# A two-way gated delta-rule scan on one core: queries, keys and state scaled ahead of the products, and sums left to PSUM

## The chip, the core and the metric

The kernel runs on one core of a Trainium2 chip. The core has a matrix engine (PE) that writes to PSUM, a vector engine (DVE), an activation engine (ACT), a third elementwise engine (POOL, which here works on SBUF tiles only) and a queue that issues transfers (SP). Each engine takes its instructions in the order in which they were written out when the program was built, and they meet at semaphores. The metric is the device time of one execution in microseconds.

## The reference

One layer of a hybrid backbone over 256 context and 1024 latent tokens of width 1024. A shared projection feeds two groups: a gated delta rule with four heads of 128, run forwards and backwards, and a neighbourhood attention with eight heads of 64. Both go through one output projection, and a gated feed-forward block follows. The change touches the recurrence of the delta rule:

```python
    def step(S, xs):
        q_i, k_i, u_i, w_i, qk_i, gam_i = xs
        v_new = u_i - jnp.einsum("bhck,bhkv->bhcv", w_i, S)
        o_i = (jnp.einsum("bhck,bhkv->bhcv", q_i * jnp.exp(gam_i)[..., None], S)
               + jnp.einsum("bhcm,bhmv->bhcv", qk_i, v_new))
        g_last = gam_i[..., -1:]
        k_dec = k_i * jnp.exp(g_last - gam_i)[..., None]
        S = S * jnp.exp(g_last)[..., None] + jnp.einsum("bhck,bhcv->bhkv", k_dec, v_new)
        return S, o_i
```

`u` is the inverse of a triangular matrix times the values, `w` the same inverse times the decayed keys. The state `S` is 128x128 for each head and direction.

## The kernel before

Tokens are cut into ten chunks of 128 (the first two are context). The forward scan takes them in order, the backward scan as 1, 0, 9, 8, ... 2; a step i of the program is one chunk of each direction, so there are ten steps with twenty chunk scans. What depends on no state was made earlier and lies in memory: `y_d` (the triangular inverse), `at_d` (decayed query-key products), keys in both layouts (`kT_d`, `k_d`), queries (`qT_d`) and values (`v_d`). `load` (L267) fetches six tiles of 256 KB for a latent chunk, for both directions at the start of the step before.

`scan` (L1181) is a generator. In each chunk it computes K S (`kT` and `s`), subtracts the values after scaling by `EG` (L1193, one DVE instruction per head), multiplies by the inverse (`vn` and `y`), scales the result twice: on ACT to `vk` for the state (L1214, one per head), and on DVE to `vn` for the output (L1216). The output is a sum of queries times state, scaled by `EG` and written out per head (L1207 on ACT when the latent chunk is met first, L1204 on DVE when it is met the second time), and of `at` times `vn` (L1223). The new state is the old one times `ET` plus `kt` times `vk` (L1233, one per head). A chunk that both directions have passed is normalised, gated and split into two parts by `finish` (L1242). Each direction's context chunks give no output, its last chunk no state.

A product of two 128x128 tiles of f32 goes to PE as two passes, so four heads show as eight instructions in the trace. PSUM holds two accumulators of 128x512 for the scan (tag `ps`) and two larger ones for the attention (tag `sc`).

Beside the scan runs the neighbourhood attention (`attention`, L287): 32 blocks of two heads, here called pairs. Of a pair, PE makes the scores (`kh`, `kl` with `qs`), DVE adds the bias and takes the maximum (L338), ACT the exponential (L341), DVE normalises (L343), PE transposes (the ten products of `bt` with `cst`), ACT copies to `pt` (L351), PE multiplies by the values (`vc`, `vw`), and ACT and DVE split the result (L363, L364). POOL clears the context columns of a bias tile `bt` (L304), and SP loads the rest (L305). A bias tile can be cleared only when its former transposes are done.

The order of the two is written out by hand. The main loop (L1303 on) asks the two scans in turn for a piece; after each piece `beside(PACE)` adds 0.72 to a count, and for each full unit of it the attention goes on by one of its yields (two per pair, 67 in all). The list so made is then put in order for each engine by a scheduler that works with modelled times. In the last step, the remaining attention and the first products of the output projection (`two_blocks`, the tiles `ew`) are written out.

## Time and profile before

| | us |
|---|---|
| median of three runs | 1526.46 |
| lowest and highest | 1523.25, 1526.57 |
| span of the profiled execution (its first to last instruction) | 1527.5 |
| PE, DVE, ACT, POOL busy in that span | 1462.8, 1013.5, 707.1, 184.1 |
| the stage in which the scan runs | 558 to 800 |

The profile shows one execution; its page gives no time for it beside the span, which is 1.0 us above the median of the runs. Matmuls and transposes are called from two helper lines (L99, L103), so the names of tiles tell them apart: `ps` are the scan's, `sc` the attention's. [...] The chain of waits follows the work that ended last back through whatever released it. A releaser named in a row is the one that came last by the profile.

### The profile page before, as it was taken

How to read it: one execution, taken by the hardware profiler on the slowest of the kernel's cores; microseconds unless marked ns; L12 is line 12 of the kernel's file. 1: busy time of each engine (PE TensorE's matmuls, PEld its weight loads, DVE VectorE, ACT ScalarE, POOL GpSimd, SP SyncE). 2: the span in 40 equal slices, each digit the busy share in tenths (PEclk: the TensorE clock that was granted, in tenths of full speed). 3: DMA queues.
4: the chain of work that ended last, by engine and by line, in shares of the span. 5: the costliest groups of instructions: out<-in, count | busy, mean ns of one | idle time of the engine just before them, and what ended most of it. 6: DMA issues, size and time to landing. Idle time of an engine off the chain costs nothing.

```text
span 1527.5 us, 23479 instructions
## 1 busy us (share of the span) xinstructions
PE 1462.8 (96%) x8365; PEld 1209.5 (79%) x8365; DVE 1013.5 (66%) x1908; ACT 707.1 (46%) x1379; POOL 184.1 (12%) x251
## 2 busy tenths in 40 slices
PE   6999998899999989999899999999999999999998
PEld 3789787678877778887787888788888888888887
DVE  4886579455687427679976488766565656599652
ACT  5443461574366536666643284333333334354441
POOL 0153500243134300000100000000000000000000
PEclk9999999999999999999999999999999999999999
DMA  9377133565477789998529404433333335798742
GB/s 368 110 235 231 58 86 122 184 179 179 131 216 252 222 266 277 279 273 247 170 65 317 166 35 163 134 104 103 104 104 103 104 104 166 252 367 288 235 152 83
DMA packets 209829, 276.28 MB, mean 181 GB/s; under 512 B 15968, under 2 KB 116912, under 8 KB 208688
## 3 DMA queue, kind: packets, MB, share of 16 engines
q1 hardware_dynamic: 208992, 274.41, 56.0%
q8 instruction: 66, 1.08, 0.3%
q14 instruction: 51, 0.42, 0.1%
q10 hardware_dynamic: 720, 0.37, 0.1%
HBM read 209.93 MB, written 68.98 MB: 183 GB/s over the span
## 4 chain that ended last, share of the span: by engine, by line
PE 65%; DVE 8%; DMA 6%; ACT 5%; issue 2%; SPq 1%; POOL 0%; POOLq 0%; ACTq 0%; DVEq 0%
PE ps L99 44%; PE blk L99 10%; PE sc L99 4%; PE pr L99 3%; DMA nv_d<-zt 2%; PE sc L103 2%; PE m L99 1%; DMA wraw<-w_nqk 1%; DMA wad<-wa 1%; ACT bt L341 1%; DVE bt L338 1%; DVE ulo L1418 1%; ACT pt L351 1%; DVE x L1587 1%; SPq L1065 0%
## 5 line engine op out<-in xcount | busy, mean ns | idle before, releaser
L99 PE MATMUL ps<-hT,uhi 128*128 128x512 f32 x496 | 146.8, 390 | 1.5 <-DVE e L1708 1.4
L99 PE MATMUL ps<-lT,uhi 128*128 128x512 f32 x496 | 146.4, 389 | 0.0
L99 PE MATMUL ps<-hT,ulo 128*128 128x512 f32 x496 | 146.2, 389 | 0.0
L99 PE MATMUL blk<-hh,whi 128*128 128x512 f32 (+1 forms) x456 | 139.1, 397 | 2.0 <-ACT hh L720 1.3
L99 PE MATMUL blk<-hh,wlo 128*128 128x512 f32 (+1 forms) x456 | 130.1, 378 | 0.0
L99 PE MATMUL blk<-hl,whi 128*128 128x512 f32 (+1 forms) x456 | 129.3, 377 | 0.0
L99 PE MATMUL ps<-hB,uhi 128*128 128x512 f32 x436 | 129.1, 390 | 0.0
L99 PE MATMUL ps<-lB,uhi 128*128 128x512 f32 x436 | 128.8, 389 | 0.0
L99 PE MATMUL ps<-hB,ulo 128*128 128x512 f32 x436 | 128.7, 389 | 0.0
L1417 ACT CAST uhi<-wq 128x512 fp32r<-128x512 f32 x101 | 60.3, 621 | 132.8 <-PE ps L99 67.7
L1417 ACT CAST uhi<-ws 128x512 fp32r<-128x512 f32 x91 | 54.7, 622 | 144.8 <-PE ps L99 77.5
L1418 DVE TENSOR_TENSOR ulo<-wq,uhi 128x512 fp32r<-128x512 f32 x101 | 67.2, 687 | 65.4 <-ACT uhi L1417 38.5
L99 PEld LDWEIGHTS ps<-hT,uhi 128*128 128x128 f32 x496 | 93.0, 188 | 21.3 <-ACT uhi L1417 1.8
L99 PEld LDWEIGHTS ps<-lT,uhi 128*128 128x128 f32 x496 | 93.0, 188 | 19.7 <-DVE lT L1571 0.5
L99 PEld LDWEIGHTS ps<-hT,ulo 128*128 128x128 f32 x496 | 93.1, 188 | 19.4
L99 PEld LDWEIGHTS ps<-hB,uhi 128*128 128x128 f32 x436 | 81.9, 188 | 17.4 <-issue 0.5
L99 PEld LDWEIGHTS ps<-lB,uhi 128*128 128x128 f32 x436 | 81.8, 188 | 17.3 <-DVE lB L1571 0.4
L99 PEld LDWEIGHTS ps<-hB,ulo 128*128 128x128 f32 x436 | 81.9, 188 | 17.0
L99 PEld LDWEIGHTS blk<-hh,wlo 128*128 128x128 f32 x456 | 80.9, 191 | 17.9 <-issue 2.5
L99 PEld LDWEIGHTS blk<-hl,whi 128*128 128x128 f32 x456 | 81.0, 190 | 15.4
L99 PEld LDWEIGHTS blk<-hh,whi 128*128 128x128 f32 x456 | 77.7, 193 | 19.4 <-ACT hh L720 3.1
L338 DVE CUSTOM_DVE_ANT_0 bt<-sc,bt 128x640 f32<-128x640 f32 x64 | 52.5, 822 | 50.3 <-issue 38.7
(337 smaller groups left out, 3073.0 us busy)
## 6 DMA issues: line engine op xcount, KB each, us to landing
wq<-w_fo SPq DMA_DIRECT2D x99, 256.0 KB
wq<-w_gu SPq DMA_DIRECT2D x88, 256.0 KB
wad<-wa SPq DMA_DIRECT2D x64, 256.0 KB
bt<-rpb SPq DMA_DIRECT2D x64, 192.0 KB
t_d<-g SPq DMA_DIRECT2D x22, 512.0 KB
fr<-t_d SPq DMA_DIRECT2D x44, 256.0 KB
f_d<-g SPq DMA_DIRECT2D x33, 256.0 KB
fr<-f_d SPq DMA_DIRECT2D x33, 256.0 KB
```

The costliest lines, as they stand in the source:

```text
L99: i = nc.tensor.matmul(*args, **kw)
L103: i = nc.tensor.transpose(*args, **kw)
L338: dve.tensor_tensor_reduce(bt, sc[:, u * 640:u * 640 + 640], bt, 1.0, -3.0e38, OP.add, OP.max, m[:, 0:1])
L341: act.activation(bt, bt, AF.Exp, bias=m[:, 1:2], accum_out=m[:, 2:3])
L351: act.copy(pt, sc[:, u * 640:u * 640 + 640])
L1417: act.copy(hi, self.raw[key])
L1418: dve.tensor_tensor(lo, self.raw[key], hi.bitcast(F32), OP.subtract)
L1587: dve.tensor_tensor(B[at][:, k], B[x][:, k], B.get(y, B["B11"])[:, k], OP.subtract)
```

## The change

The recurrence is written in another way. `w`, the inverse times the decayed keys, is made as a tile of its own one step ahead (`before`): POOL scales the keys by `EG` to `ke`, PE multiplies `ke` with `y`, ACT copies the result with its sign turned to `w`. In the scan, `y` times `v` and `w` times `s` then add up in one accumulator `z`, and one DVE instruction scales it by `B` for all four heads to `vn`, which serves both the output and the state. POOL also scales the keys by `KD` (in place), the queries by a row of decays `er` (which SP loads broadcast over partitions and ACT exponentiates) and the state by `ET` to `sd`. Queries times state and `at` times `vn` add up in one accumulator. The tables `KN` and `KB`, the loads of `kT` and the tile `vk` go. The state tile of a direction is one buffer that is written over.

The forward scan's pieces are written out before the backward scan's, `before` for the next step beside them, and `finish` as a third party; each piece says by its yield how much it counts, and PACE is 1.25. Values and `at` of the next step are fetched between the two scans. Buffers: `kt`, `y`, `qT` four, `er` two, `at` three.

```diff
-PACE = 0.72
+PACE = 1.25
...
+        kt, y = (own.tile([128, 4, 128], F32, name=n, tag=f"{n}{d}") if own else
+                 scan_in.tile([128, 4, 128], F32, name=n, tag=n, bufs=4) for n in ("kt", "y"))
+        sp.dma_start(fl(kt), k_d[c * 128:(c + 1) * 128])
+        sp.dma_start(y, y_d[d, c])
+        qT = er = None
+        if c >= 2:
+            qT, er = (scan_in.tile([128, 4, 128], F32, name=n, tag=n, bufs=2 if n == "er" else 4)
+                      for n in ("qT", "er"))
+            u = (d * NCH + c) * 4
+            sp.dma_start(fl(er), g_d[u:u + 4].rearrange("h t -> (h t)").partition_broadcast(128))
+            sp.dma_start(qT, qT_d[:, :, (c - 2) * 128:(c - 1) * 128])
+        ready[d, c] = kt, qT, er, y
+
+    def load_values(d, c, own=None):
...
-                KN, KB = (fw.tile([128, 2, NCH, 4], F32, name=n, tag=n, bufs=1) for n in ("KN", "KB"))
-                dve.tensor_tensor(KN, KD, NB, OP.mult)
-                dve.tensor_tensor(KB, KD, B, OP.mult)
...
+        def before(d, c):
+
+            kt, qT, er, y = ready[d, c]
+            carried = c != ORDER[d][0]
+            if carried:
+                ke = work("ke", 1)
+                pool.tensor_tensor(ke, kt, spread(EG, d, c), OP.mult)
+            if c >= 2:
+                act.activation(er, er, AF.Exp)
+                pool.tensor_tensor(qT, qT, er, OP.mult)
+            yield 0.0
+            if carried:
                 p = bank()
                 for h in range(4):
-                    pe.matmul(p[:, hs[h]], kT[:, h], s[:, h], start=True, stop=True)
+                    pe.matmul(p[:, hs[h]], ke[:, h], y[:, h], start=True, stop=True)
+                made[d, c] = w = work("w")
+                act.activation(fl(w), p, AF.Copy, scale=-1.0)
+            if c != last[d]:
+                pool.tensor_tensor(kt, kt, spread(KD, d, c), OP.mult)
+            yield 0.5
+
+        def scan(d, c):
+            kt, qT, er, y = ready.pop((d, c))
+            v, at = values_of.pop((d, c))
+            lat, s = c >= 2, S[d]
+            vn = work("vn")
+            z = bank()
+            for h in range(4):
+                pe.matmul(z[:, hs[h]], y[:, h], v[:, h], start=h == 0, stop=s is None, skip_group_check=True)
+            if s is not None:
+                w = made.pop((d, c))
+                if c != last[d]:
+                    sd = work("sd", 1)
+                    pool.tensor_tensor(sd, s, spread(ET, d, c), OP.mult)
                 for h in range(4):
...
+                    pe.matmul(z[:, hs[h]], w[:, h], s[:, h], start=False, stop=True, skip_group_check=True)
+            dve.tensor_tensor(vn, z.rearrange("p (h i) -> p h i", h=4), spread(B, d, c), OP.mult)
             if lat:
                 p = bank()
                 for h in range(4):
-                    pe.matmul(p[:, hs[h]], at[:, h], vn[:, h], start=True, stop=True)
-                dve.tensor_tensor(o, p.rearrange("p (h i) -> p h i", h=4), o, OP.add)
+                    pe.matmul(p[:, hs[h]], qT[:, h], s[:, h], start=h == 0, stop=False, skip_group_check=True)
+            yield 1.0
+            if lat:
+                for h in range(4):
+                    pe.matmul(p[:, hs[h]], at[:, h], vn[:, h], start=False, stop=True, skip_group_check=True)
+                o = oacc[:, c - 2]
+                if c in seen:
+                    dve.tensor_tensor(fl(o), p, fl(o), OP.add)
+                else:
+                    act.copy(fl(o), p)
             if c != last[d]:
                 p = bank()
                 for h in range(4):
-                    pe.matmul(p[:, hs[h]], kt[:, h], vk[:, h], start=True, stop=True)
...
+                    pe.matmul(p[:, hs[h]], kt[:, h], vn[:, h], start=True, stop=True)
+                if s is None:
+                    S[d] = s = work("s%d" % d, 1)
+                    act.copy(fl(s), p)
+                else:
+                    dve.tensor_tensor(fl(s), p, fl(sd), OP.add)
...
+            def both():
+                yield from scan(0, ORDER[0][i])
+                if i + 1 < NCH:
+                    for d in range(2):
+                        load_values(d, ORDER[d][i + 1])
+                yield from scan(1, ORDER[1][i])
+
+            main = both()
+            live = [main]
+            if i + 1 < NCH:
+                live.append(chain(*(before(d, ORDER[d][i + 1]) for d in range(2))))
+            while live or ending:
+                live += ending
+                ending.clear()
                 nxt = []
...
+                for g in live:
+                    n = next(g, None)
+                    if n is not None:
                         nxt.append(g)
...
+                        beside(PACE * n)
```

How the instructions move is shown at three places. On DVE in an early step, before (`vn` and `s` are the scan's, `mx`, `bt` and `na` the attention's):

```order
L1233 SCALAR_TENSOR_TENSOR s_6148<-s_5854,ET,ps 128x128
L342 RECIPROCAL mx<-mx 128x1
L340 TENSOR_SCALAR mx<-mx 128x1
L1233 SCALAR_TENSOR_TENSOR s_6148<-s_5854,ET,ps 128x128
L343 TENSOR_SCALAR bt<-bt,mx 128x640
L1233 SCALAR_TENSOR_TENSOR s_6148<-s_5854,ET,ps 128x128
L342 RECIPROCAL mx<-mx 128x1
L1233 SCALAR_TENSOR_TENSOR s_6148<-s_5854,ET,ps 128x128
L343 TENSOR_SCALAR bt<-bt,mx 128x640
L364 TENSOR_TENSOR na_4919<-sc,na_4919 128x8x16
L1193 SCALAR_TENSOR_TENSOR vn<-ps,EG,v 128x128 x4
```

and of the change (L349 to L354 are the softmax's lines there):

```order
L354 TENSOR_SCALAR bt<-bt,mx 128x640
L1232 TENSOR_TENSOR vn<-ps,B 128x512
L353 RECIPROCAL mx<-mx 128x1
L354 TENSOR_SCALAR bt<-bt,mx 128x640
L375 TENSOR_TENSOR na_4911<-sc,na_4911 128x8x16
L1254 TENSOR_TENSOR s_4986<-ps,sd 128x512
L349 ISA bt,mx<-sc,bt 128x640
```

Where four pieces of the state stood between the pieces of a softmax, one instruction for four heads stands now.

On PE in an early step of the change, from the products that make `w` to the first product that reads `vn`; rows of the attention's scores and value products are left out:

```order
L100 MATMUL ps<-y,ke 128x128
L104 MATMUL sc<-cst,bt 128x128 x5
L100 MATMUL ps<-y,ke 128x128
...
L100 MATMUL ps<-y,ke 128x128 x2
...
L100 MATMUL ps<-v,y 128x128 x4
L100 MATMUL ps<-s_5070,w 128x128 x4
L100 MATMUL ps<-s_5070,qT 128x128 x4
L104 MATMUL sc<-cst,bt 128x128 x5
...
L100 MATMUL ps<-vn,at 128x128
```

The product `ke` times `y` belongs to the next step; the three products after it stand together, and transposes of the attention lie between the last of them and the products that read `vn`.

On POOL, in the same stretch of the change, where before a row of 54 clears of `bt` stood alone (`L304 MEMSET bt 128x256 x54`):

```order
L1229 TENSOR_TENSOR sd<-s_5070,ET 128x512
L315 MEMSET bt 128x256
L1202 TENSOR_TENSOR ke<-kt,EG 128x512
L1214 TENSOR_TENSOR kt<-kt,KD 128x512
L1205 TENSOR_TENSOR qT<-qT,er 128x512
L315 MEMSET bt 128x256 x2
L1205 TENSOR_TENSOR qT<-qT,er 128x512
L1229 TENSOR_TENSOR sd<-s_4986,ET 128x512
```

Clears of bias tiles, which wait for the attention's transposes, now stand between the scan's scalings.

103 lines of the change are left out of this document (31 added, 72 removed).

## The prediction

> **What bounds the kernel now.** I read first the busy time by stage (columns: stretch, its length, then busy us and instructions of PE, weight loads, DVE, ACT and POOL, granted clock, DMA share, GB/s). All edits lie in the stage from 558 to 800 us, where the recurrence of the scans ("scan" below) runs beside 32 pairs of attention blocks. Behind it PE is busy 99%.
>
> ```profile
> 558.00:800.00 242.00, 224.77 (x2039) 191.66 (x2038) 191.56 (x687) 151.44 (x412) 21.98 (x62) 1.00 0.78 222
> 830.00:1527.00 697.00, 692.09 (x3060) 571.31 (x3058) 451.04 (x712) 275.53 (x470) 0.00 (x0) 1.00 0.46 156
> ```
>
> PE looks 93% full here, which would leave 17 us. The groups of the stage and pieces of the chain of waits (start, us, what) say otherwise:
>
> ```profile
> L99 PE MATMUL ps<-vn,y 128*128 128x128 f32 x144 | 21.3, 283 | 0.8 <-DVE vn L1216 0.5 <-ACT oacc L1207 0.3
> 754.75 1.79 PE ps L99 x16
> 758.25 0.55 PE sc L103 x5
> 668.57 1.79 PE sc L99 x26
> 787.30 7.85 PE sc L99 x34
> ```
>
> A scan product is recorded with 283 ns, yet sixteen pass in 1.79 us, 0.112 each: the rest is pipeline. By this pace the stage needs, of PE: 688 scan products x 0.112 = 77; a pair takes ten transposes (2 x 0.55), twenty value and six score products (1.79) and four more score products (about 0.5), 3.4 us, x 32 = 109; 48 products of the output projection x 0.231 = 11; 32 transposes x 0.11 = 4. That is 201 us: PE waits 41 of 242, not 17. DVE is at 79%, the next fullest.
>
> Where the waits lie, the steps of the scan show (step 2 to step 8, one row each, same columns), and the chain inside one early and one late step:
>
> ```profile
> 594.00:617.40 23.40, 22.38 (x200) 18.98 (x200) 16.16 (x54) 14.21 (x40) 1.76 (x6) 1.00 1.07 300
> 617.40:640.30 22.90, 22.33 (x200) 18.90 (x200) 16.32 (x54) 14.01 (x40) 2.05 (x7) 1.00 0.95 267
> 640.30:665.00 24.70, 24.15 (x216) 20.82 (x216) 17.30 (x56) 15.26 (x43) 1.97 (x7) 1.00 0.90 263
> 665.00:688.20 23.20, 21.54 (x201) 18.74 (x202) 18.40 (x62) 12.10 (x29) 1.94 (x6) 1.00 1.08 284
> 688.20:721.10 32.90, 29.44 (x288) 25.24 (x287) 30.51 (x117) 22.05 (x61) 3.11 (x10) 1.00 0.85 246
> 721.10:754.70 33.60, 30.22 (x291) 25.44 (x290) 30.49 (x118) 22.69 (x62) 3.70 (x11) 1.00 0.66 193
> 754.70:785.00 30.30, 27.61 (x266) 23.36 (x266) 27.87 (x108) 18.94 (x51) 3.85 (x8) 1.00 0.32 92
> ```
>
> ```profile
> by line: PE ps L99 38.4%; PE sc L99 24.2%; ACT oacc L1207 10.0%; ACT bt L341 8.5%; PE sc L103 8.4%; ACT pt L351 5.6%; ACT vk L1214 3.7%; issue 3.6%
> 632.33 1.10 PE ps L99 x8
> ...
> 633.72 0.62 ACT oacc L1207 x2
> ...
> 636.25 0.81 ACT bt L341 x2
> ...
> 638.16 0.82 ACT bt L341 x2
> ...
> 639.24 1.04 ACT oacc L1207 x4
> ...
> 640.32 0.38 PE ps L99
> by line: PE ps L99 25.5%; PE sc L99 24.3%; PE sc L103 16.5%; DVE bt L338 5.7%; ACT pt L351 5.6%; issue 3.3%; ACT vk L1214 3.1%; PE ps L103 3.0%; DVE bt L343 2.7%; DVE oacc L1204 2.3%; ACT bt L341 1.6%; DVE s L1233 1.5%; POOL bt L304 1.0%; D
> ```
>
> The first "by line" row is 617.4 to 640.4, the second 729.4 to 763. Early, 71% of a step (16.3 of 23 us) is PE; from 633.4 on, PE waits for ACT, which carries eight `oacc` and eight `vk` evictions, one per head, among the exponentials. Late, 69% (23.3 of 33.6) is PE and DVE is busy 91%. So neither engine is full for long; the waits come where a scan eviction in pieces and the attention's softmax share a queue.
>
> **The change part by part.** The groups that fall and those by which the new ones are priced:
>
> ```profile
> L1193 DVE SCALAR_TENSOR_TENSOR vn<-ps,EG,v 128x128 f32<-128x128 f32 x72 | 21.5, 341 | 1.2 <-PE ps L99 1.1
> L1233 DVE SCALAR_TENSOR_TENSOR s<-s,ET,ps 128x128 f32<-128x128 f32 x64 | 19.0, 342 | 3.8 <-PE ps L99 3.7
> L1204 DVE SCALAR_TENSOR_TENSOR oacc<-ps,EG,oacc 128x128 f32<-128x128 f32 x32 | 9.8, 341 | 0.0
> L1223 DVE TENSOR_TENSOR oacc<-ps,oacc 128x512 f32<-128x512 f32 x16 | 11.0, 687 | 5.9 <-PE ps L99 5.9
> L1216 DVE TENSOR_TENSOR vn<-ps,NB 128x512 f32<-128x512 f32 x16 | 10.9, 684 | 1.0 <-ACT vk L1214 0.8
> 691.58 1.12 DVE L1233 SCALAR_TENSOR_TENSOR s<-s,ET,ps 128x128 f32<-128x128 f32 x4 [0.17 <-PE ps L99]
> L1214 ACT ACTIVATE vk<-ps,KN 128x128 f32<-128x128 f32 x64 | 19.4, 373 | 3.1 <-PE ps L99 3.1
> L1207 ACT ACTIVATE oacc<-ps,EG 128x128 f32<-128x128 f32 x32 | 9.8, 392 | 2.5 <-PE ps L99 2.5
> L1263 ACT CAST gah<-z 128x512 fp32r<-128x512 f32 x8 | 4.9, 613 | 7.4 <-DVE z L1262 7.3
> L1288 POOL TENSOR_TENSOR ew<-ew 128x512 fp32r<-128x512 f32 x2 | 2.6, 1282 | 3.3 <-ACT ew L1287 3.3
> L304 POOL MEMSET bt<- 128x256 f32 x60 | 19.4, 324 | 212.9 <-PE sc L103 139.1 <-PE sc L99 22.1 <-DMA qs<-nq_d 6.7
> SPq L305 <- PE sc L103: 26.7, 30, 2.8
> ```
>
> DVE: 168 pieces go, four in 1.12 us, so 47 us, and 32 whole tiles, 22; there come 20 `vn`, 16 state updates and 8 output sums, 44 x 0.69 = 30. DVE falls by 39 us, from 79% to 63% of the stage.
>
> ACT: 104 pieces, about 31 us, go; 18 `w`, 16 exponentials of `er`, 8 output and 2 state copies come, 44 x 0.61 (a 128x512 cast) = 27. The exponentials are off the path, a step ahead. Only the pieces' dispatch and their place among the softmax change.
>
> PE: the 72 products of keys and state give way to 72 of `w` and state; 72 products `ke` x `y`, two passes each, are new: 144 x 0.112 = 16.1 us, on the engine that carries most of the chain. This is the price.
>
> POOL: 18 `ke`, 18 `kt`, 16 `qT` and 16 `sd` tiles, 68 x 1.28 = 87 us, beside 19 us of clearing bias tiles: 44% of the stage, and all one step ahead except `sd`. Inside a step `sd` has as cover the products and eviction of `vn` of its own chunk (16 products, 1.8 us, and 0.69), and a step is 22 us while a chunk's own recurrence (`w` products 0.9, `vn` 0.7, `kt` products 0.9, state 0.7) is about 3.5. If POOL were late by more than that cover, the state update would wait, and behind it on DVE the next softmax.
>
> DMA: 20 loads of `kT` go, 16 of `er` come, 256 KB each: 1 MB less of 54 MB (222 GB/s x 242 us), four SP issues fewer. Costed at nothing: SP's longest wait in the scan (the last row: total, times, longest) is for a bias buffer that PE still reads, not for an issue; four buffers for `kt`, `y`, `qT` cover the earlier start.
>
> PACE: attention advances per `beside` unit. Before, an early step makes 8 x 0.72 = 5.76 calls and a late one 14 x 0.72 = 10.1; now 5 x 1.25 = 6.25 and 6 x 1.25 = 7.5; two calls are a pair.
>
> The sum, against the profiled 1527.5 us (1.0 above the median of the runs, within their spread), step by step. I assume that half of the chain's waits stay; the bounds are all and none.
> - Steps 3 to 5: PE 16.3 + 16 products x 0.112 = 1.8 + a quarter pair, 0.8 = 18.9; waits 6.7, half is 3.3: 22.2 each, 66.6 for 70.8: -4.2.
> - Steps 6 to 8: PE 23.3 + 1.8 - 1.29 pairs x 3.4 = 20.7; waits 10.3, half 5.2: 25.9 each, 77.7 for 96.8: -19.1.
> - Step 2: 2.6 us of added work against a wait of 6.74 us for a bias load (below): 0.
> - Steps 0 and 1: 1.2 pairs and 32 products more, 7.7; half falls into a wait of 4.91 us that stays (below): +3.9.
> - Step 9: attention has 67 calls; 63.3 were made before it, now 60, so 1.65 pairs more run there, 5.6, and 1 us of their own wait: +6.6.
>
> Together -12.8. The same half taken on the whole stage gives less: 201 + 16.1 + 20.5 = 238 for 242, -4. The steps know where the waits are, the stage counts all of PE's work; I take a value between, nearer the steps: **-10, 1517 us**.
>
> ```profile
> 600.41 6.74 DMA bt<-rpb
> 553.58 4.91 DMA zT_d<-zt
> ```
>
> The recorded PE time alone would give another sum: 17 us idle, 16 filled, so 1 us of gain at most. [...]
>
> **The rivals.**
>
> *The attention keeps its waits, and the new products come on top (slower).* Place: PE's queue, where transposes stand for the softmax on DVE and value products for the copy on ACT. For it: ACT sheds only 4 us, and early steps wait as much with DVE at 71% as late ones at 91%. Against: ACT's own evictions in the early chain go, and the added products lie in those waits. The assumed waits of steps 3 to 8 are 3 x 6.7 + 3 x 10.3 = 51 us; every tenth more that stays costs 5. From -10 the sign turns when more than 0.7 of them stay; at nine tenths it is +10, **1537 us**.
>
> *POOL's queue sets the step.* Its tensor products share something with DVE:
>
> ```profile
> 169.91 1.05 POOL L877 TENSOR_TENSOR rc<-GH,cst 128x512 fp32r<-128x512 f32 x1
> ...
> 173.36 2.22 DVE L899 TENSOR_TENSOR WK<-WK,cst 128x1280 f32<-128x1280 f32 x1
> 174.19 2.29 POOL L877 TENSOR_TENSOR rc<-GL,cst 128x512 fp32r<-128x512 f32 x1
> ```
>
> Alone 1.05, beside a DVE product of two SBUF tiles 2.29. At 2.29, eight per step and six bias clears are 20.3 us, under 22; clears also hold the queue until old transposes are done (139.1 us of waiting in the row of L304). With 0.7 us more per instruction the step is 26: +4 x 6, **1541 us**. Against it: of DVE's scan instructions now all read PSUM, not two SBUF tiles.
>
> [...]
>
> *The early half is DMA's.* The DMA share is 0.90 to 1.08 in steps 2 to 5, with 263 to 300 GB/s. If those cannot shrink, 66.6 becomes 70.8: -6, **1521 us**. Against: one bias load alone stands on the chain.
>
> *It does not do what it says*: scan and attention were independent, attention's chain sets the pace, the added products fill gaps: **1527 us**.
>
> **How the numbers follow.** Forecast 0.58, waits stay 0.15, DMA 0.12, no effect 0.08, POOL 0.07. A measurement of this kernel tells about 0.3% (4.6 us) from no change. Faster: 0.54 of the forecast's, 0.06 of DMA's, 0.01 else, 0.61; same: 0.04, 0.06, 0.06, 0.02, 0.18; slower 0.21. With no waits left in steps 3 to 8 it would be 25 less than with half, which PE's own 217 us forbid before 1503; with nine tenths 1537. The range is 1503 to 1534; the forecast's own 1507 to 1522.
>
> **What would show it.** Right: steps 6 to 8 of 24 to 27 us where 30 to 34 stood; steps 3 to 5 of 21 to 23; DVE near 153 us and PE's need by pace (217 us) at 0.93 of the stage. `ke` and `sd` on POOL near 1.3 us. Wrong: DVE, ACT or PE idle before `ps` with POOL as releaser; early steps of 24 or more with transposes waiting for `bt`; `er` or `at` loads on the chain; or a tail after the last scan product of more than 6 us without PE work.

## The result and the profile after

The changed kernel takes 1544.8 us (median of 4 runs, 1539.78 to 1545.63), the kernel before 1524.86 us (4 runs). The ratio is 1.0127, with a 95% interval of 1.0105 to 1.0149: the change makes the kernel 16 to 23 us **slower**, where 10 us faster was forecast. The profiled execution took 1544.56 us (span 1542.4). That of the kernel before has a span of 1527.5, above all four of its times, so the profiles show about 5 us less of the loss than the medians.

All of what the profiles show lies in the stage of the scans. The busy time by step, from the first whole-tile `vn` eviction of a step (L1232; before, L1216) to that of the next (columns: stretch, its length, then busy us and instructions of PE, weight loads, DVE, ACT and POOL, granted clock, DMA share, GB/s), steps 2 to 9, first the changed kernel:

```profile
592.10:616.30 24.20, 22.54 (x219) 20.28 (x218) 13.55 (x38) 13.59 (x28) 9.47 (x13) 1.00 0.93 269
616.30:645.50 29.20, 26.64 (x240) 23.79 (x239) 16.40 (x46) 15.72 (x32) 14.41 (x19) 0.94 0.86 245
645.50:670.10 24.60, 22.49 (x218) 20.45 (x218) 14.97 (x38) 14.22 (x30) 10.78 (x14) 1.00 0.93 274
670.10:692.50 22.40, 22.36 (x218) 20.45 (x217) 13.49 (x39) 12.00 (x26) 10.38 (x14) 1.00 1.01 264
692.50:726.60 34.10, 28.15 (x266) 24.44 (x266) 27.52 (x85) 20.25 (x53) 11.43 (x16) 1.00 0.64 192
726.60:758.70 32.10, 27.70 (x265) 24.05 (x264) 26.82 (x81) 16.82 (x48) 10.17 (x15) 1.00 0.59 182
758.70:785.20 26.50, 25.57 (x246) 22.44 (x245) 23.35 (x80) 16.96 (x48) 6.61 (x10) 1.00 0.41 123
785.20:814.90 29.70, 28.99 (x221) 24.51 (x220) 18.46 (x64) 12.39 (x37) 0.62 (x2) 1.00 0.15 41
```

The same marks in the kernel before:

```profile
593.40:616.80 23.40, 22.14 (x201) 18.73 (x199) 16.16 (x54) 14.21 (x39) 2.00 (x6) 1.00 1.07 299
616.80:639.70 22.90, 22.38 (x203) 18.95 (x202) 16.32 (x55) 14.01 (x39) 2.00 (x6) 1.00 0.95 271
639.70:659.60 19.90, 19.53 (x169) 16.66 (x170) 14.15 (x47) 11.02 (x31) 1.69 (x5) 1.00 0.90 259
659.60:682.90 23.30, 21.31 (x205) 18.90 (x205) 17.44 (x58) 13.21 (x34) 1.95 (x6) 1.00 1.04 272
682.90:715.80 32.90, 29.44 (x281) 24.66 (x280) 30.34 (x118) 21.65 (x61) 3.11 (x10) 1.00 0.89 255
715.80:749.50 33.70, 30.60 (x294) 25.91 (x292) 30.48 (x118) 22.73 (x62) 3.11 (x10) 1.00 0.73 220
749.50:780.80 31.30, 28.33 (x273) 23.81 (x274) 29.60 (x116) 20.73 (x57) 4.74 (x9) 1.00 0.37 104
780.80:799.80 19.00, 19.00 (x121) 16.23 (x121) 13.26 (x47) 6.90 (x24) 0.00 (x0) 1.00 0.05 15
```

Compare the lengths: steps 3 to 5 grew from 66.1 to 76.2 us, steps 6 to 8 fell only from 97.9 to 92.7, and the last stretch grew from 19.0 to 29.7. With +0.8 in step 2 and -1.3 up to it that makes 15.1 us; the two spans differ by 14.9. In the last stretch PE is busy nearly all the time, before and after (19.0 of 19.0 and 29.0 of 29.7 us): there stands work that was moved, not a stall.

The groups of the stage, in the changed kernel (the last columns are busy us, mean ns, then idle time before and what ended it):

```profile
L354 DVE TENSOR_SCALAR bt<-bt,mx 128x640 f32<-128x640 f32 x64 | 42.5, 663 | 0.7
L1205 POOL TENSOR_TENSOR qT<-qT,er 128x512 f32<-128x512 f32 x16 | 20.6, 1291 | 50.3 <-DMA qT<-qT_d 24.9 <-DVE s L1254 6.5 <-DMA er<-g_d 6.4
L1202 POOL TENSOR_TENSOR ke<-kt,EG 128x512 f32<-128x512 f32 x17 | 18.9, 1109 | 11.9 <-PE ps L100 11.9
L1229 POOL TENSOR_TENSOR sd<-s,ET 128x512 f32<-128x512 f32 x16 | 16.9, 1058 | 11.7 <-DVE s L1254 9.5 <-DMA z<-zT_d 1.2 <-DVE mx L353 1.0
L1204 ACT ACTIVATE er<-er 128x512 f32<-128x512 f32 x16 | 10.1, 629 | 20.3 <-DMA er<-g_d 20.3
L201 DVE TENSOR_TENSOR nwt<-orr 128x4 f32<-128x4 f32 x24 | 5.3, 223 | 0.5
```

Three things are to be seen. ACT stood 20.3 us for loads of `er`, and POOL 50.3 us at the `qT` products, half of it for loads of `qT`. The normalisation of the softmax, which the change does not touch, takes 663 ns where it took 556 (x64, 7 us), and the small instructions of `finish` grew alike (L201: 223 ns for 157). And `ke` and `sd` themselves are as quick as hoped, 1.1 us. The two DVE groups in the kernel before, where L201 was L200:

```profile
L343 DVE TENSOR_SCALAR bt<-bt,mx 128x640 f32<-128x640 f32 x64 | 35.6, 556 | 0.5
L200 DVE TENSOR_TENSOR nwt<-orr 128x4 f32<-128x4 f32 x24 | 3.7, 157 | 0.1
```

What a wait for `er` does is in the timeline of step 3 (start, us, engine, line, what; in brackets the idle time before and what ended it):

```profile
626.83 0.37 SPq L279 DMA_DIRECT2D er<-g_d  x1
...
632.48 0.63 ACT L1204 ACTIVATE er<-er 128x512 f32<-128x512 f32 x1 [4.43 <-DMA er<-g_d]
633.01 0.25 ACT L374 CAST na<-sc 128x128 fp32r<-128x128 f32 x1
...
633.29 0.29 DVE L375 TENSOR_TENSOR na<-sc,na 128x128 fp32r<-128x128 f32 x1 [3.64 <-ACT na L374]
...
633.64 0.27 PE L100 MATMUL sc<-kh,qs 128*128 128x256 f16 x1 [2.46 <-DVE na L375]
```

The load was issued 5.6 us before it was there; the exponential was already at the head of ACT's queue. The attention's own eviction `na` (0.25 us) stood behind it, DVE stood for `na`, and PE for DVE. In the chain of waits of the late steps the same load stands ahead of two small chains of DVE (start, us, what):

```profile
692.32 5.37 DMA er<-g_d
...
700.36 0.88 DVE nwt L1270
...
704.81 0.89 DVE nwt L201
...
707.47 0.69 DVE vn L1232
```

### The profile page after: what moved, and what is told of

It reads as the page before. It is cut to its first block, busy times and chain, and to the rows that moved or that the text cites. A ratio compares the mean times of both kernels' runs of the same rounds, so it can differ in the third digit from the quotient of the medians.

```text
span 1542.4 us, 23567 instructions
## 1 busy us (share of the span) xinstructions
PE 1474.1 (96%) x8509; PEld 1224.7 (79%) x8509; DVE 998.2 (65%) x1750; ACT 700.9 (45%) x1311; POOL 259.3 (17%) x319
## 4 chain that ended last, share of the span: by engine, by line
PE 46%; DVE 6%; ACT 2%; DMA 2%; issue 1%; SPq 0%; DVEq 0%; ACTq 0%
PE ps L100 42%; PE sc L100 2%; PE sc L104 1%; DMA wad<-wa 1%; DVE bt L349 1%; DVE ulo L1457 1%; DVE x L1626 1%; DVE x L1602 0%; DMA wraw<-w_out 0%; DVE lT L1597 0%; DMA er<-g_d 0%; DVE acc L254 0%; DMA wq<-w_gu 0%; DVE bt L354 0%; DVE ws L1452 0%
## 5 line engine op out<-in xcount | busy, mean ns | idle before, releaser
L100 PEld LDWEIGHTS ps<-lT,uhi 128*128 128x128 f32 x496 | 93.4, 189 | 19.9 <-DVE lT L1610 0.4
L349 DVE CUSTOM_DVE_ANT_0 bt<-sc,bt 128x640 f32<-128x640 f32 x64 | 52.6, 823 | 68.3 <-PE sc L100 56.2
```

The costliest lines, as they stand in the source:

```text
L100: i = nc.tensor.matmul(*args, **kw)
L349: dve.tensor_tensor_reduce(bt, sc[:, u * 640:u * 640 + 640], bt, 1.0, -3.0e38, OP.add, OP.max, m[:, 0:1])
```

## The experiments

Times are medians; the ratio is to the kernel before on the same chip, with its 95% interval. "us" of a ratio are (ratio - 1) x 1525. Each engine's order comes from a scheduler that works with modelled times, so an edit may reorder engines far from it; where PE's and DVE's orders stayed, it is said. GpSimd is another name of POOL. In the edits shown, dots stand for lines left out.

### The price of the added products

**no_ke_products**

```diff
-                p = bank()
-                for h in range(4):
-                    pe.matmul(p[:, hs[h]], ke[:, h], y[:, h], start=True, stop=True)
                 made[d, c] = w = work("w")
-                act.activation(fl(w), p, AF.Copy, scale=-1.0)
+                act.activation(fl(w), fl(ke), AF.Copy, scale=-1.0)
```

> The changed kernel without the 72 products ke x y (144 passes): ACT copies ke itself into w, so ACT's count of instructions, POOL's work, the loads and the order of everything else stay. Left out: the part of w that y gives. Theory P (the price): the added products come on top because the stage keeps about 40 us of waits of PE, so taking away 144 x 0.112 = 16 us of PE's need gives nearly all of it back: 1527 to 1531. Theory D (late loads of er hold ACT's and POOL's queues) and theory C (GpSimd's tensor products hold up DVE): PE would only wait longer at the same places, 1538 to 1543.

Measured: 1527.2 us, ratio 1.0014 (0.9998 to 1.0029): 17 us less than the changed kernel, as theory P says.

**before_plus_products**

```diff
             p = bank()
+            if s is not None:
+                for h in range(4):
+                    pe.matmul(p[:, hs[h]], kt[:, h], y[:, h], start=True, stop=True)
             for h in range(4):
                 pe.matmul(p[:, hs[h]], y[:, h], r[:, h], start=True, stop=True)
```

> The kernel before with 72 products of keys and y (144 passes, 16.1 us of PE by pace) added in front of the y products, into the same PSUM bank, which these overwrite; nothing else changed. Theory W: the waits of PE keep their size and the products come on top, 14 to 17 us slower, 1538 to 1542. The prediction's view (added products lie in the waits, half of them free): 6 to 9 us slower, 1530 to 1534. All free: 1522 to 1528.

Measured: 1540.9 us, ratio 1.0105 (1.0080 to 1.0131): 16 us. PE waited 41 us of this stage and yet, within the interval (12 to 20 us), no part of 16.1 us of new work fell into those waits. From both sides the term is right, 16 to 17 us, and it comes on top in full. In neither run did the orders stay: in the traces about an eighth of DVE's instructions of the stage stand at another place in no_ke_products, and about a fifth in before_plus_products. So neither run has the products alone, and what speaks for the size is that two different forms agree on it.

### GpSimd beside DVE

**no_pool_scaling**

```diff
-                ke = work("ke", 1)
-                pool.tensor_tensor(ke, kt, spread(EG, d, c), OP.mult)
+                ke = kt
...
-                pool.tensor_tensor(qT, qT, er, OP.mult)
...
-                pool.tensor_tensor(kt, kt, spread(KD, d, c), OP.mult)
...
-                    pool.tensor_tensor(sd, s, spread(ET, d, c), OP.mult)
...
-                    dve.tensor_tensor(fl(s), p, fl(sd), OP.add)
+                    dve.tensor_tensor(fl(s), p, fl(s), OP.add)
```

> The changed kernel without any of the 68 tensor products on GpSimd (ke, kt, sd, qT); the loads, the exponentials of er, the products on PE and DVE's additions stay. Left out: all scalings of keys, queries and state. Theory C: DVE's normalisations of the softmax fall from 663 ns back to about 556 and the small instructions of the ends of chunks from 230 to 330 ns to about 160, DVE's busy time in the stage falls by some 10 us and the time by 8 to 14: 1531 to 1537. Theory P: 0 to 4 less. Theory D: 3 to 6 less, since POOL's queue no longer stands for qT but ACT's still does for er.

Measured: 1535.1 us, ratio 1.0062 (1.0041 to 1.0083): 10 us less than the changed kernel; the normalisations are back at 555 ns. That is within what theory C said, but the runs on `er` below show that 6 to 7 of the 10 belong to the `qT` products, and most of that to a wait and not to contention.

**before_plus_pool**

```diff
+            spread = lambda t: t[:, d, c].rearrange("p (h o) -> p h o", o=1).to_broadcast([128, 4, 128])
+            scr = work("scr", 1)
+            if s is not None:
+                pool.tensor_tensor(scr, kt, spread(EG), OP.mult)
+                if c != last[d]:
+                    pool.tensor_tensor(scr, s, spread(ET), OP.mult)
+            if c != last[d]:
+                pool.tensor_tensor(scr, kt, spread(KD), OP.mult)
+            if lat:
+                pool.tensor_tensor(scr, qT, y, OP.mult)
```

> The kernel before, with the 68 tensor products of GpSimd added and nothing else: they read the same keys, state and queries and write a scratch tile that nobody reads. Theory C: 6 to 12 us slower, 1531 to 1537, normalisations 620 ns or more in place of 556. Theories P and D: within 3 us of the kernel before, 1522 to 1529.

Measured: 1543.7 us, ratio 1.0125 (1.0106 to 1.0144): 19 us, more than any theory said, with the order of PE, DVE and ACT the same row for row. Steps 2 to 5 keep their lengths (23.4, 22.9, 19.9, 23.7 us); the loss is in steps 6 and 7, whose busy times by stretch are, with the group of the normalisation:

```profile
683.50:723.00 39.50, 32.95 (x285) 28.05 (x285) 34.75 (x117) 21.74 (x61) 12.13 (x18) 0.87 0.71 206
723.00:763.20 40.20, 32.88 (x294) 27.79 (x293) 37.02 (x117) 22.72 (x62) 14.68 (x20) 0.92 0.61 184
...
L343 DVE TENSOR_SCALAR bt<-bt,mx 128x640 f32<-128x640 f32 x64 | 41.2, 644 | 0.5
```

DVE does its 117 instructions (117 and 118 before) in 34.75 and 37.02 us in place of 30.34 and 30.48, and the steps grow by 6.6 and 6.5. In early steps, where DVE is at about 70%, GpSimd's products cost next to nothing; where DVE is at 91%, they hold it up, and the clock falls on top (last section). At a granted clock of 0.87 and 0.92 the two steps lose an estimated 5.1 and 3.2 us of PE's full speed, so how much of their 13 us is DVE's and how much the clock's was not separated. In the changed kernel the same products cost less (below); there the late steps hold fewer attention pairs, DVE is at 81 and 84%, and the clock is 1.00. That this is the reason is argued, not shown.

### What er costs

**no_er**

```diff
-            sp.dma_start(fl(er), g_d[u:u + 4].rearrange("h t -> (h t)").partition_broadcast(128))
...
-                act.activation(er, er, AF.Exp)
-                pool.tensor_tensor(qT, qT, er, OP.mult)
```

> The changed kernel without the 16 loads of er, their exponentials on ACT and the 16 qT products on POOL. Left out: the decay of the queries. Theory D: these waits (ACT for er 20 us in 11 places, POOL at qT for qT and er 31 us) are on the path of transposes and scores; without them 10 to 15 us less, 1530 to 1535, and steps like the one from 616 to 645 us fall from 29 to 24. Theory P: 0 to 3 less, 1541 to 1545. Theory C: a quarter of POOL's products goes, 2 to 4 less.

Measured: 1528.1 us, ratio 1.0023 (1.0008 to 1.0038): 16 us less, with PE's order nearly that of the changed kernel. Theory D's size; but the price of the products had claimed as much, and both cannot be the whole of 19 us. So the next runs take `er` apart.

**er_later**

```diff
-                act.activation(er, er, AF.Exp)
-                pool.tensor_tensor(qT, qT, er, OP.mult)
+            if d == 1:
+                decay(0)
             yield 0.0
...
+            if d == 1:
+                decay(1)
             yield 0.5
```

(`decay(d)` holds the two instructions; `decay(0)` stands where the second direction begins.)

> The changed kernel with the same work; only the exponentials of er on ACT and the qT products on POOL come later in the step: those of the first direction stand where the second direction's ke products begin, those of the second behind its w and kt. Nothing is left out. Theory D (the time went to ACT and POOL standing in their queues for loads of er and qT that were issued 4 to 6 us before): the waits of ACT for er (20 us) and of POOL at qT (50 us) fall to less than a third and most of the 17 us that leaving er out gave come back: 1530 to 1536. Theory L (it is the load on ACT, POOL and the DMA queues that er brings, not its place): 1541 to 1546. Theory W (the waits belong to the attention and only the 16 us of products came on top): 1541 to 1546 too.

Measured: 1544.3 us, ratio 1.0117 (1.0091 to 1.0143). This run says nothing of the place: the scheduler gave every engine the order of the changed kernel row for row. It is a repeat of it, no more.

**er_load_only**

```diff
-                act.activation(er, er, AF.Exp)
-                pool.tensor_tensor(qT, qT, er, OP.mult)
```

> The changed kernel with the 16 loads of er, but without their exponentials and without the qT products; nothing reads what is loaded. Left out: the decay of the queries. If the loads cost by the DMA queues they fill (4 MB and 16 issues on SP), most of the 17 us that leaving all of er out gave stay: 1538 to 1544. If they cost only by the instructions that wait for them (ACT's queue behind the exponential, POOL's behind the product), it is like the run without er: 1526 to 1531.

Measured: 1527.4 us, ratio 1.0019 (1.0005 to 1.0033), like the run without `er`. The 4 MB cost nothing by themselves; what costs is who waits for them.

**er_no_load**

```diff
-            sp.dma_start(fl(er), g_d[u:u + 4].rearrange("h t -> (h t)").partition_broadcast(128))
...
-                act.activation(er, er, AF.Exp)
+                act.activation(fl(er), cst[:, :512], AF.Exp)
```

> The changed kernel with the exponentials and the qT products, but without the 16 loads of er: the exponential reads a constant tile that has been in SBUF from the start, so ACT never waits for a load there. Left out: the right decay of the queries. If ACT's waits for er are what costs: 1528 to 1534. If it is the work of the two instructions (10 us on ACT, 21 us on POOL beside DVE): 1538 to 1545. POOL's waits at qT for the load of qT itself (25 us) stay in either case.

Measured: 1544.0 us, ratio 1.0122 (1.0105 to 1.0139). On the numbers it speaks for work; its trace says otherwise. With two buffers the exponential now waits for POOL to have read the `er` before the last, and POOL stands for `qT`:

```profile
POOL qT L1203 <- DMA qT<-qT_d: 24.7, 5, 9.4
ACT er L1202 <- POOL qT L1203: 18.7, 10, 3.9
```

ACT stood 18.7 us in 10 waits, as long as for the load. The wait had only changed its name, so the run does not decide.

**product_of_er**

```diff
-                pool.tensor_tensor(qT, qT, er, OP.mult)
+                pool.tensor_tensor(er, er, er, OP.mult)
```

> The changed kernel with the qT product on GpSimd replaced by one of the same size that reads er alone (er times er, in place); the loads of qT and er and the exponentials stay, and the order of instructions on PE and DVE is that of the changed kernel row for row. Left out: the decay of the queries. If POOL's standing for the load of qT (25 us in 8 waits, with sd, ke, kt and the clearing of bias tiles queued behind it) is what costs: 1528 to 1534, like the run without er. If the work of the product beside DVE costs: 1541 to 1546. ACT's waits for er (20 us) stay in either case.

Measured: 1539.9 us, ratio 1.0083 (1.0061 to 1.0104), orders on PE and DVE as in the changed kernel. Between the two expectations: POOL's standing for `qT` costs 6 to 7 us.

**er_exp_only**

```diff
-                pool.tensor_tensor(qT, qT, er, OP.mult)
```

> The changed kernel with the loads of er and their exponentials, but without the qT product; the order on PE and DVE is that of the changed kernel row for row. Left out: the decay of the queries. If ACT's standing for er (20 us in 11 waits) is what costs, most of the loss stays: 1538 to 1545. If the product on POOL is what costs (its wait or its work): 1526 to 1532. With the run that replaces the product: product's wait alone when both come out near 1530, product's work when this one does and the other stays at 1544.

Measured: 1538.3 us, ratio 1.0078 (1.0058 to 1.0098), again with the same orders. The product's own work is worth about 1 us, inside the intervals. What remains against er_load_only, 1.0078 to 1.0019, is 9 us, and ACT's wait is still there:

```profile
ACT er L1204 <- DMA er<-g_d: 18.8, 10, 3.3
```

**exp_ready**

```diff
-            sp.dma_start(fl(er), g_d[u:u + 4].rearrange("h t -> (h t)").partition_broadcast(128))
...
-                act.activation(er, er, AF.Exp)
-                pool.tensor_tensor(qT, qT, er, OP.mult)
+                act.activation(fl(er), cst[:, :512], AF.Exp)
```

> The changed kernel with the 16 exponentials of er on ACT, but taken from a constant tile that lies in SBUF, without the loads of er and without the qT product; 22 of 4020 rows of PE's order differ. Left out: the decay of the queries. Beside the run with loads and exponentials (1538) and the run with loads alone (1527): if ACT's standing for the load costs the 11 us between them, 1526 to 1531; if the exponentials' own 10 us of ACT cost it, 1535 to 1540.

Measured: 1527.7 us, ratio 1.0022 (1.0011 to 1.0034). All sixteen exponentials run, but not in their places: having nothing to wait for, they were all put first, at 553.7 to 572.6 us in the trace, where er_exp_only has them from 562.9 to 702.6. So this run shows that they cost nothing where ACT is free; it does not tell their work from their wait. The traces of er_exp_only and er_load_only, with PE's and DVE's orders the same but for a few rows, do. From 553 us to the end of step 8 (first er_exp_only, then er_load_only):

```profile
553.00:780.60 227.60, 208.27 (x1984) 184.60 (x1982) 158.40 (x470) 133.14 (x308) 72.44 (x108) 1.00 0.79 229
553.00:771.40 218.40, 207.61 (x1977) 184.18 (x1976) 157.09 (x470) 125.74 (x292) 72.18 (x108) 1.00 0.84 238
```

PE is busy for as long, and stands 19.3 us in place of 10.8. Six stands of PE, of 1.1 to 2.2 us and 9.5 us together, come with the six exponentials that ACT waited for longest (1.6 to 3.3 us each). At the other ten, which take the same 0.63 us and waited 1.1 us at most, PE never stood for more than 0.3 us, up to 1.5 us past their ends. So the 9 us are ACT standing in its queue for a load, and not ACT's work; the traces say so, no run has the exponentials in place on ready data.

### With all prices away

**no_er_no_pool** (the edits of no_er and no_pool_scaling together)

```diff
-                act.activation(er, er, AF.Exp)
-                pool.tensor_tensor(qT, qT, er, OP.mult)
...
-                pool.tensor_tensor(ke, kt, spread(EG, d, c), OP.mult)
...
-                pool.tensor_tensor(kt, kt, spread(KD, d, c), OP.mult)
...
-                    pool.tensor_tensor(sd, s, spread(ET, d, c), OP.mult)
```

> The changed kernel with neither er (loads, exponentials) nor any tensor product on GpSimd; PE's products, DVE's and ACT's whole-tile instructions, order and pacing stay. Left out: all scalings of keys, queries and state. The prediction's assumption, half of PE's waits go when the evictions become whole tiles, tested without GpSimd and er: about 1517 if the two costs are independent of each other (17 and 10 us off 1545). Theory W (the waits of PE in the stage, 40 us, belong to the attention): not under 1526.

Measured: 1524.9 us, ratio 0.9996 (0.9982 to 1.0009): the time of the kernel before, 8 us above the first expectation and 1 us under the second's bound. The costs of `er` and GpSimd overlap in the `qT` product: after `er`, the other GpSimd products are worth 4 us.

**bare** (no_er_no_pool and no_ke_products together)

```diff
-                    pe.matmul(p[:, hs[h]], ke[:, h], y[:, h], start=True, stop=True)
...
-                act.activation(fl(w), p, AF.Copy, scale=-1.0)
+                act.activation(fl(w), fl(ke), AF.Copy, scale=-1.0)
```

> The changed kernel without er, without any tensor product on GpSimd and without the 72 products ke x y: what is left of the change is the whole-tile evictions, the accumulation in PSUM and the pacing, with PE's need at the 201 us of before. Left out: all scalings, and the part of w that y gives. If the price of the products adds to the rest one to one, as in the kernel before: 1525 - 16 = 1507 to 1511, and the whole-tile instructions themselves are worth some 16 us. If the products had filled waits here: 1517 to 1525.

Measured: 1512.5 us, ratio 0.9901 (0.9880 to 0.9922): 14 to 15 us less again. So what is left of the change, whole-tile evictions, accumulation in PSUM and pacing, is worth 15 us (12 to 18). Its steps 6 to 9, from an execution of 1507.24 us, 5 below the median, so that they flatter it:

```profile
669.60:698.40 28.80, 26.77 (x259) 22.97 (x258) 24.12 (x85) 18.30 (x49) 2.77 (x8) 1.00 0.75 202
698.40:726.80 28.40, 26.33 (x247) 22.52 (x246) 24.14 (x86) 17.97 (x49) 2.76 (x8) 1.00 0.64 196
726.80:753.10 26.30, 23.89 (x223) 19.79 (x222) 22.32 (x76) 15.97 (x46) 4.30 (x8) 1.00 0.43 134
753.10:782.70 29.60, 28.89 (x220) 24.41 (x219) 18.77 (x64) 12.31 (x36) 0.62 (x2) 1.00 0.14 41
```

The late steps are 83.5 us against 92.7 with the prices and 97.9 before. The last stretch is 29.6 here too: it is the pacing's, whatever the scans cost.

### Parts alone, and other versions

**before_pace_0_85**

```diff
-PACE = 0.72
+PACE = 0.85
```

> The kernel before with the attention paced at 0.85 in place of 0.72 calls per unit, so that it ends in step 8 rather than in step 9; no other edit, nothing left out. The change's own pacing moves pairs the other way, out of steps 6 to 8 into step 9. If the place of a pair costs nothing as long as PE needs the same (201 us) and waits the same: 1523 to 1528. If late steps, with DVE over 90% busy, pay more for a pair than early ones or the tail: slower by 3 us or more here, 1528 to 1536, from the steps 6 to 8; if they pay less, faster by 3 or more.

Measured: 1529.5 us, ratio 1.0033 (1.0018 to 1.0048): 5 us slower, but not from the late steps. By the same marks, in an execution 3 us above the median, steps 2 to 5 took 101.1 us for 89.5, steps 6 to 8 94.5 for 97.9. An early step makes 8 x 0.13 = 1.04 calls more, half a pair, so four take 2.1 pairs more for 11.6 us: 5.5 a pair where PE needs 3.4. It is the early steps that have no room. The expectation named the wrong half.

**kt_ahead_act**

```diff
+            if c != last[d]:
+                for h in range(4):
+                    act.activation(kt[:, h], kt[:, h], AF.Copy, scale=sc(KD, h))
...
-            vk = work("vk")
-            if c != last[d]:
-                for h in range(4):
-                    act.activation(vk[:, h], p[:, hs[h]], AF.Copy, scale=sc(KN if sg is NB else KB, h))
-            if lat:
+            if lat or c != last[d]:
                 dve.tensor_tensor(vn, p.rearrange("p (h i) -> p h i", h=4),
...
-                    pe.matmul(p[:, hs[h]], kt[:, h], vk[:, h], start=True, stop=True)
+                    pe.matmul(p[:, hs[h]], kt[:, h], vn[:, h], start=True, stop=True)
```

> The kernel before with one part of the change alone, without GpSimd, er or products on PE: the keys kt are scaled by KD at the start of the chunk (by ACT, four pieces, from SBUF), so that the product with the keys takes vn from DVE's one whole-tile eviction and the 64 pieces vk of ACT go. Nothing is left out. PE, loads and pacing as before; DVE gets four whole tiles more (2.7 us). If PE's waits come from scan evictions in pieces that stand on the chain beside the softmax: 5 to 10 us faster, 1515 to 1520. If ACT's load is what counts, not the place: 1523 to 1527.

Measured: 1525.1 us, ratio 1.0007 (0.9993 to 1.0021): no difference. The 72 `vk` evictions in pieces leave the scan's own chain, and nothing is gained. The run is not clean: the 72 new pieces stand 6.8 us of the stage at the head of ACT's queue for loads of `kt`, and a gain could hide behind that. But in the trace of the kernel before PE waits for `vk` only once, 1.0 us, so by themselves these pieces were hardly what PE waited for.

**finish_on_act**

```diff
-            dve.tensor_tensor(o, o, r.rearrange("p (h o) -> p h o", o=1).to_broadcast([128, 4, 128]), OP.mult)
+            for h in range(4):
+                act.activation(o[:, h], o[:, h], AF.Copy, scale=r[:, h:h + 1])
```

> The kernel before with one DVE instruction of each end of a chunk (the scaling of oacc by its norm, 0.69 us x 8, all in the late steps) moved to ACT as four pieces of a head; nothing is left out. If DVE's work bounds the late steps (91% busy, and they took all of what GpSimd's products cost): 4 to 6 us faster, 1518 to 1521. If the late steps are bound by chains across engines: 1523 to 1527.

Measured: 1527.8 us, ratio 1.0020 (1.0005 to 1.0034): 3 us slower, not faster. Taking 5.5 us off DVE's late work gives nothing, which speaks against a DVE that is 91% busy being by itself the bound of these steps. It does not settle it: the chain across engines became longer by four ACT instructions, which could cost what DVE gains; that was not tested.

**undo_queries**

```diff
...
+                for h in range(4):
+                    sc = EG[:, d, c, h:h + 1]
+                    if c in seen:
+                        dve.scalar_tensor_tensor(o[:, h], p[:, hs[h]], sc, o[:, h], op0=OP.mult, op1=OP.add)
+                    else:
+                        act.activation(o[:, h], p[:, hs[h]], AF.Copy, scale=sc)
             yield 1.0
             if lat:
+                p = bank()
                 for h in range(4):
-                    pe.matmul(p[:, hs[h]], at[:, h], vn[:, h], start=False, stop=True, skip_group_check=True)
...
+                    pe.matmul(p[:, hs[h]], at[:, h], vn[:, h], start=True, stop=True)
+                dve.tensor_tensor(fl(o), p, fl(o), OP.add)
```

(The loads and exponentials of `er` and the `qT` products go as in no_er.)

> The changed kernel with the query part undone: no er, no qT product on GpSimd; the products of queries and state go to a bank of their own and are scaled at their eviction in four pieces, as before the change (ACT on first visits, DVE on second), and the at products are added by one DVE instruction of 0.69 us. Nothing is left out. Against the run without er: 8 x 4 ACT pieces for 8 copies (+5 us of ACT), on DVE 8 x 4 pieces and 8 whole tiles more (14.5 us), 16 banks more. If the late half is bound by DVE, half to all of these 14 us show: 1533 to 1542. If the late half is bound by waits between engines and not by DVE's work: 1527 to 1532.

Measured: 1531.6 us, ratio 1.0044 (1.0026 to 1.0061). With the full output it regains 13 us of the change's loss; the old query evictions, in pieces, cost 3 us against no `er` at all, which is inside the intervals, so DVE's 14.5 us of added work are mostly hidden: the second expectation. It is still 7 us slower than the kernel before.

**keys_by_rows**

```diff
+            act.activation(erow[:2 * NU], rows[:2 * NU], AF.Exp)
+            sp.dma_start(ge_d, erow[:2 * NU])
...
-                ke = work("ke", 1)
-                pool.tensor_tensor(ke, kt, spread(EG, d, c), OP.mult)
+                pool.tensor_tensor(kT, kT, er, OP.mult)
...
+                    pe.matmul(p[:, hs[h]], kT[:, h], s[:, h], start=True, stop=True)
+                r = vn
+                dve.tensor_tensor(fl(r), fl(v), p, OP.subtract)
```

> A version without two of the three prices, output complete: exp(g) is stored once, in rows, when the decay tables are made, so that er comes ready and ACT has no exponential of it; GpSimd scales the transposed keys kT by er in place of making ke; PE takes kT x state, DVE subtracts it from v in one whole tile, and y and vn are multiplied as before the change, so that the 72 products ke x y (16 us of PE) and the w evictions go. In exchange 18 whole tiles more on DVE (12 us), one product and one eviction more in each chunk's own chain, 20 loads of kT. From 1544: -16 for the products, -11 for ACT's wait. If DVE's 12 us fall into its idle time: 1516 to 1522, faster than before. If the late steps pay them and the longer chain: 1524 to 1532.

Measured: 1539.9 us, ratio 1.0101 (1.0075 to 1.0127), far above both expectations. POOL now stands for `kT`, late in place of `er`:

```profile
POOL kT L1208 <- DMA kT<-kT_d: 31.3, 10, 7.6
```

Step 3 took 30.9 us, steps 6 and 7 36.5 each, in an execution 6 us above the median. Which of that wait, DVE's added work and the longer chain weighs most was not separated. No version tried beats the kernel before.

## Why the prediction was wrong, point by point

The step that failed is the one that took the new small work off the path: the loads of `er` and `qT`, ACT's exponentials and POOL's products were costed at nothing, and the waits for those loads cost 15 us. One term was also too large: fewer of PE's waits went than the half that was assumed, which makes some 7 us of benefit too many. The price was right.

In ratios to the kernel before, the runs make one ladder from the changed kernel (1.0127, its repeat 1.0117; taken as 1.0122) down: without POOL's wait for `qT` 1.0083, without that product 1.0078, without ACT's wait for `er` 1.0019, without the loads 1.0023, without the other GpSimd products 0.9996, without the `ke` products 0.9901. In us: 6 + 1 + 9 + 0 + 4 + 14, 34 in all, of which 19 lie above the kernel before and 15 below it. Each rung is known to 3 to 5 us by the intervals, and depends on the order in which the parts were taken away: GpSimd's products were worth 10 us before `er` went and 4 after.

- **"16.1 us, the price": right.** 16 us added to the kernel before, 17 and 14 us taken from two forms of the changed one. PE's need by pace was the right measure of it. Each of the three is known to about 4 us.
- **"I assume that half of the chain's waits stay": in the changed kernel, all stayed.** Steps 3 to 5 took 76.2 us for a need of 3 x 18.9, which leaves 19.5 us of waits where 3 x 6.7 = 20 stood; steps 6 to 8 took 92.7 for 3 x 20.7, which leaves 30.6 for 31. (The prediction took its steps between other marks; by the marks used here the waits before were 17 and 28, so they even grew.) But they were not the same waits. Without prices the change is worth 15 us, where the sum had -10 - 16.1 = -26. Of these 11 us some 4 are the last stretch's (below); the other 7 say that the evictions in pieces held fewer of the waits than half. kt_ahead_act points the same way for the `vk` evictions, one of the two named on the chain. What the waits that stay hang on is open.
- **"The exponentials are off the path, a step ahead" and "DMA ... costed at nothing": wrong, and here is the largest mistake of mechanism.** The use was moved a step ahead, and the load was not. `er` and `qT` are fetched in the step in which `before` reads them, so the instructions stand at the heads of ACT's and POOL's queues for transfers that took 5.4 and 5.6 us in the two views above. Four buffers for `kt`, `y` and `qT` covered the place where a load lands, not when it is issued, and `er` has two. The prediction put the cost at nothing; the runs put it at 9 us for ACT and 6 for POOL. The prediction did name "`er` or `at` loads on the chain" as a sign against it, and the chain of waits shows `er` there.
- **POOL: 87 us "all one step ahead except `sd`".** `sd` was never late. POOL was busy 92.6 us of the stage, where 87 + 19 = 106 were forecast, and was not the bound; `qT` took 1.29 us, `ke` and `sd` 1.1. Its products other than `qT` cost 4 us (1 to 7), by the longer DVE instructions most likely through DVE.
- **DVE "near 153 us": 175.** The pieces went as counted, but 7 us came back in the normalisations (663 for 556 ns) and 8 in the small instructions of `finish`; the other 7 were not traced.
- **Steps 0, 1 and 9.** Forecast +3.9 and +6.6, measured -1.3 and +10.7 us. In the last stretch ACT copies `pt` six times for two, so three pairs run there in place of one: 2 pairs x 3.4 = 6.8 us, where the sum had 1.65, and the rest is scan products that also moved. PE is full there, so this is the price of pacing, and it stands in the run without the other prices too.
- **The rivals.** "The attention keeps its waits" came nearest in size, 1537 us for 1544.8, with all in place of nine tenths staying. Half of its mechanism holds: the products came on top in full. The other half does not: the added waits are not the attention's own, since the time falls by 15 us when ACT and POOL wait for no `er` and no `qT`, with the attention unchanged. "POOL's queue" had its place right (behind POOL's products) and its cause wrong: POOL's products were not stretched to 2.29 us (the longest of the stage took 1.54), they stood for data (50.3 us at `qT`) and stretched DVE's instructions (663 for 556 ns). "The early half is DMA's": the loads of `er` that nobody waited for cost nothing measurable (er_load_only 1.0019, no_er 1.0023). "It does not do what it says" falls.

- **The signs named.** Steps 6 to 8 were to take 24 to 27 us: 34.1, 32.1 and 26.5. Steps 3 to 5 were to take 21 to 23: 29.2, 24.6 and 22.4. PE's need was to be 0.93 of the stage: 217 of 257 is 0.84. Early steps of 24 and more and `er` on the chain came as the signs against; POOL as releaser of `ps` and a tail without PE work did not.

So -10 became +19 by 9 us of ACT's wait, 6 of POOL's, 1 of the `qT` products' work, 4 of GpSimd beside DVE and 11 of a benefit that was counted too high, less 2 because the price is 14 on this ladder. That these add up to 29 proves nothing, since the 11 are what was left over; the price had been counted right.

## What to carry to other kernels

When a step is computed one step ahead, ask whether its loads move too: if the transfer stays where it was, the wait lands in the queue of an engine that others need, where 0.25 us of their work stands behind it. Fetching two steps ahead is the remedy that follows; no run here tried it. Waiting time of the busiest engine is not by itself room for new work: of 16 us of products added to a PE that waited 41 us, nothing measurable was free. To price a moved operation, run it with and without its work, with and without its wait, and look whether the engines' order stayed: one run here changed nothing (er_later), and one moved the very instructions that it was to test (exp_ready).

## What the runs showed of the hardware

**Beside a GpSimd product, a DVE instruction of 0.16 us took 0.93 us and ended with it.** From the timeline of the changed kernel, the same two kinds of DVE instruction, with a GpSimd product beside them and without:

```profile
711.55 0.54 DVE L354 TENSOR_SCALAR bt<-bt,mx 128x640 f32<-128x640 f32 x1
...
712.84 1.04 POOL L1229 TENSOR_TENSOR sd<-s,ET 128x512 f32<-128x512 f32 x1 [1.98 <-DVE s L1254]
...
713.63 0.85 DVE L354 TENSOR_SCALAR bt<-bt,mx 128x640 f32<-128x640 f32 x1
...
717.01 1.04 POOL L1214 TENSOR_TENSOR kt<-kt,KD 128x512 f32<-128x512 f32 x1
...
717.14 0.93 DVE L201 TENSOR_TENSOR nwt<-orr 128x4 f32<-128x4 f32 x1
...
720.58 0.16 DVE L201 TENSOR_TENSOR nwt<-orr 128x4 f32<-128x4 f32 x1
```

A product of 128x4 numbers, of an SBUF tile with itself, takes 0.93 us in place of 0.16, and ends at 718.07, when POOL's product ends (718.05). The normalisation takes 0.85 us in place of 0.54. The whole of the longer time is counted as DVE's busy time (0.93 us). What holds the instruction up the traces do not show, only that it began 0.13 us after POOL's product and that the two ends lie 0.02 us apart. What the prediction had not seen is that the victims are tiny instructions in a serial chain.

**After two long stalls of PE the granted clock was lower, 0.56 and 0.50.** The stall of 2.46 us above is followed by a lower granted clock (changed kernel, columns as in the first view; the clock is the third from the end):

```profile
631.00:633.60 2.60, 0.17 (x2) 0.00 (x1) 0.29 (x1) 1.12 (x3) 0.11 (x1) 1.00 1.05 351
633.60:635.60 2.00, 1.96 (x12) 1.80 (x12) 0.75 (x2) 0.89 (x2) 1.41 (x2) 0.56 0.72 214
635.60:637.60 2.00, 2.00 (x12) 1.64 (x11) 0.23 (x3) 1.51 (x3) 1.07 (x2) 0.59 0.37 90
```

For 4 us PE ran at 0.56 to 0.59, by these rows an estimated 1.7 us of full-speed work lost, on a stall of 2.5. In the kernel before with GpSimd's products, PE stands for 3.31 us up to 700.34 us and then runs for 8 us at half clock, of which the first instruction, the first row and the last:

```profile
700.34 1.30 PE L103 MATMUL sc<-cst,bt 128*128 128x128 f32 x5 [3.31 <-DVE bt L343]
...
700.00:702.00 2.00, 1.33 (x6) 1.09 (x7) 2.00 (x8) 1.06 (x3) 1.39 (x2) 0.50 0.02 5
...
706.00:708.00 2.00, 2.00 (x17) 1.67 (x14) 1.32 (x6) 0.99 (x3) 0.00 (x0) 0.50 0.11 33
```

The steps of the kernel before, 593.4 to 799.8 us, all show 1.00. The length of a stall alone does not tell what follows it: ahead of the scans, at the same work, PE stands for 1.83 us up to 194.68 us in the kernel before, and the next 2 us show 0.61; in the changed kernel it stands for 1.84 us up to 194.63 us, and the next 2 us show 1.00. The longest stall of the stage in the kernel before, 1.86 us up to 563.84 us, is followed by 1.00 too. So it may pay to break up a wait as long as the two above even where its total stays; no run tried that.
